# Multi-query attention on one core: first loads swapped between two queues, products of zeros on TensorE before the value products, and another cut of the last head pair

## The chip, the cores and the metric

One core of a Trainium2 chip runs the whole kernel. The metric is the time of one execution on the device in microseconds. The engines are TensorE (PE in the profile, its weight loads PEld), ScalarE (ACT), VectorE (DVE), GpSimd (POOL) and SyncE (SP). ScalarE, SyncE and GpSimd can also issue DMA transfers, each on a queue of its own.

## The reference

Eight batches, 1024 positions, 16 query heads of 64 dimensions, and one key and one value head shared by all 16 (multi-query attention). Everything is float32 in and out.

```python
q = q.transpose(0, 2, 1, 3)                       # q: (8, 1024, 16, 64)
scores = np.matmul(q, k.transpose(0, 1, 3, 2)) / np.sqrt(head_dim)
weights = np.exp(scores - np.max(scores, axis=-1, keepdims=True))
weights = weights / np.sum(weights, axis=-1, keepdims=True)
attn_out = np.matmul(weights, v)                  # k, v: (8, 1024, 64), for every head
return attn_out.transpose(0, 2, 1, 3)
```

## The kernel before

**Units of work.** Two heads of one batch make a pair, so there are 64 pairs (`NP`). A pair has eight key tiles of 128 keys (`NKT`) and two halves `c` of 512 queries. One *score* (`score`, L576) is a key tile against one half of the queries: two matmuls (L580), one for each head, on the upper and lower 64 rows of the array, into one of three PSUM slots, `sc0` to `sc2`. An exponential then reads the slot and writes fp16 weights. ScalarE does it in one instruction of 1024 elements to a partition (`exp_act`, L600). For two key tiles of most pairs (a *duo*, 54 in all) VectorE does it instead: it reads the slot with L608 (`fixed`; the planner calls it "z"), and computes a polynomial on the bits afterwards (`poly`, L626 to L643), with help from GpSimd (L652) and, in all but a few duos, from a DMA that adds (L664).

**Value products.** `value` (L671) multiplies the weights with v, in blocks of 128 queries of one head: 16 blocks in a pair (`NB`), one matmul of 128x65 for each block and key tile (L690). v has a column of ones, so the 65th column of the result is the sum of the weights. The blocks of all pairs stand in one row and are cut into groups of seven (`grouped`, L59), which are accumulated in the PSUM banks `acc0` and `acc1`; the last pair is cut by itself, into 6, 5 and 5 blocks. When a group is complete, VectorE takes the reciprocals of the sums (L699) and multiplies (L709) into `osb` in SBUF. When all 16 blocks of a pair are there, SyncE's queue sends them out as one transfer of 512 KB (L726). In the last pair nothing is sent behind the first group; after the second the first half of the rows is sent on SyncE's queue, and after the third the second half on ScalarE's (L724), 256 KB each.

**Order.** `plan` (L86) steps through a model of the engines, with a duration for each kind of work from the constants at the head of the file, and writes a list of operations in order of its model's time. The kernel emits the list as it stands, so each engine's program order is fixed. PE's next operation is chosen at L248 to L308: a score if a slot is free or will be soon (a wait of under `WAIT`, 0.5; the slot's time gets `WAKE`, 0.27, on top), else a value product. No value product is taken until the scores are `LAG`, 1.7 pairs, ahead. `nv` counts the value products so far, and `st` is the model's start of the score.

**The start.** Pair 0's keys and queries don't go through GpSimd's queue as the others do. `load_first` (L532) loads k in two halves on SyncE's queue (L539; a row of 1 KB to a partition) and q in two halves on ScalarE's (L541; four rows of 512 bytes to a partition). `cast_first(0)` (L550) casts k's first half to fp16 twice side by side on VectorE (L554), and q's first half on ScalarE (L556). `turn_first(0)` (L560) transposes both on TensorE into the banks `acc0` and `acc1` (L566, L570); VectorE copies k out (L568), ScalarE q (L572). `cast_first(1)` and `turn_first(1)` do the same with the second halves on VectorE alone (L558, L574); `turn_first(1)` stands behind the second score in TensorE's order. The third score is the first of VectorE's duo 0; it takes key tile 6, which lies in k's second half.

Of the kernel before, what the change touches and what calls it, by code (L numbers as in the profile page):

```python
# [17 lines left out]
P = 128  # L18
# [21 lines left out]
QLEAD = 3.3  # L40
LATE = 2
STOP = 1.0
REM = (4, 3, 3, 2)
Z_GAP, Z_PE, Z_ACT = 2, 2.0, 1.0
ACC_L = 0.15
# [11 lines left out]


def grouped(NP):  # L59
    cuts = list(range(0, NB * (NP - 1) + 1, NG)) + [NB * (NP - 1) + x for x in (6, 11, 16)]  # L60
    res = []
    for a, b in zip(cuts, cuts[1:]):
        segs = []
        while a < b:
            e = min(b, a // NB * NB + NB)
            segs.append((a // NB, a % NB, (e - 1) % NB + 1))
            a = e
        res.append(tuple(segs))
    return res
# [16 lines left out]
def plan(NP, NKT, stats=None):  # L86
# [85 lines left out]
    while todo_g or groups:  # L172
        if pe <= dve:
# [95 lines left out]
            if do == "qk":  # L269
                s = min(range(3), key=lambda s: slot[s])  # L270
                st = aq if slot[s] <= aq else slot[s] + WAKE
                pe, mode = st + QK_P, "qk"
                if kind == "z":
                    d, i = vunits.pop(0)
                    slot[s] = FAR
                    zs.append((st + PE_Z, s, (d, i)))
                    gap = 0
                    emit(st, "qk", duos[d][i // 2], i % 2, s)
                else:
                    u = units.pop(0)  # L280
                    na += 1
                    act = max(act, st + PE_L)
                    emit(act, "act", *u)
                    slot[s] = act + ACT_L
                    ready[u] = act + ACT_R
                    act += ACT_P
                    gap += 1
                    emit(st, "qk", *u, s)
            elif do == "av":
                st = aa  # L290
                grp, n, j = pick
                k, segs, left, a = grp
                gp, lo, hi = segs[n]
                nb = hi - lo
                pe = st + AV_B * nb
                mode = "av"
                nv += nb
                emit(st, "av", k, segs[n], j, len(left) == NKT * len(segs), a)
                left.remove((n, j))
                used[NKT * gp + j] += nb  # L300
                if not left:
                    acc[a] = FAR
                    r = pe - AV_B + PE_R
                    evs += [(r, k, segs, a, "rec"), (r, k, segs, a, "norm")]
                    groups.remove(grp)
            else:
                nxt = [x for x in slot + acc + [tav] if T < x < FAR] + [dve] * (dve > T)
                pe = max(min(nxt, default=0.0), T + 1e-3)  # L308
# [77 lines left out]
def kernel(  # L386
# [105 lines left out]
    def of_pair(x, n):  # L492
        return x[:, NKT * n : NKT * (n + 1), :]
# [38 lines left out]
    def load_first():  # L532

        st = kst.setdefault(0, {})
        st["kn"] = osb[:, 0:NKT, :]
        st["qf"] = osb[:, NB : 2 * NB, :].rearrange("p (c h) d -> p c (h d)", h=2)
        for c in range(NQC):
            x = slice(HT * c, HT * c + HT)
            nc.sync.dma_start(  # L539
                out=st["kn"][:, x, :], in_=k[0].rearrange("(p c) d -> p c d", p=P)[:, x, :])  # L540
            nc.scalar.dma_start(  # L541
                out=st["qf"][:, x, :],
                in_=q[0, :, 0:2, :].rearrange("(c p) h d -> p c (h d)", p=P)[:, x, :],
            )
        st["k16"] = osb[:, 2 * NB : 2 * NB + NKT, :].bitcast(FP16).rearrange("p c (r d) -> p c r d", r=2)
        st["k2t"] = kvp.tile([P, NKT + 1, P], FP16, tag="k2t", name="k2t0")[:, 0:NKT, :]
        place_q(0)
        load_q(0)

    def cast_first(c):  # L550
        st = kst[0]
        x = slice(HT * c, HT * c + HT)
        for r in range(2):
            nc.vector.tensor_copy(out=st["k16"][:, x, r, :], in_=st["kn"][:, x, :])  # L554
        if c == 0:
            nc.scalar.copy(out=qn[0, 0][:, x, :], in_=st["qf"][:, x, :])  # L556
        else:
            nc.vector.tensor_copy(out=qn[0, 0][:, x, :], in_=st["qf"][:, x, :])  # L558

    def turn_first(c):  # L560
        st = kst[0]
        x = slice(HT * c, HT * c + HT)
        kps = psp.tile([P, HT, P], FP16, tag="acc0", name=f"kps{c}")
        qps = psp.tile([P, HT, P], FP16, tag="acc1", name=f"qps{c}")
        for i in range(HT):
            nc.tensor.transpose(  # L566
                kps[:, i, :], st["k16"][:, HT * c + i, :, :].rearrange("p r d -> p (r d)"), ident)
        nc.vector.tensor_copy(out=st["k2t"][:, x, :], in_=kps)  # L568
        for i in range(HT):
            nc.tensor.transpose(qps[:, i, :], qn[0, 0][:, HT * c + i, :], ident)  # L570
        if c == 0:
            nc.scalar.copy(out=of_pair(qt[0], 0)[:, x, :], in_=qps)  # L572
        else:
            nc.vector.tensor_copy(out=of_pair(qt[0], 0)[:, x, :], in_=qps)  # L574

    def score(t, c, s):  # L576
        p, j = divmod(t, NKT)
# [9 lines left out]
    def score_act(t, c, s):  # L587
        score(t, c, s)
        if t not in wt:
            wt[t] = wtp.tile([P, 2, S], FP16, tag="wt", name=f"wt{t}")  # L590
# [110 lines left out]
    def normalise(k, segs):  # L701
        a, r = acc.pop(k), rec.pop(k)
        x = segs[0][0] * NB + segs[0][1]
        e = segs[-1][0] * NB + segs[-1][2]
        n = 0
        while x < e:
            y = min(e, (x // (OSB * NB) + 1) * OSB * NB)
            m = y - x
            behind["dve"] = nc.vector.tensor_tensor(  # L709
                out=osb[:, x % (OSB * NB) : x % (OSB * NB) + m, :], in0=a[:, n : n + m, 0:D],  # L710
                in1=r[:, n : n + m].unsqueeze(2).broadcast_to([P, m, D]),
                op=ALU.mult,
            )
            x, n = y, n + m
        half = NKT // 2
        for p, lo, hi in segs:
            left[p] -= hi - lo
            b, hp = divmod(p, HP)
            o = out[b, :, 2 * hp : 2 * hp + 2, :].rearrange("(c p) h d -> p c (h d)", p=P)
            s = NB * (p % OSB)  # L720
            x = osb[:, s : s + NB, :].rearrange("p (c h) d -> p c (h d)", h=2)
            if p == NP - 1 and lo > 0:
                c = slice(half, NKT) if hi == NB else slice(0, half)
                (nc.scalar if hi == NB else nc.sync).dma_start(out=o[:, c, :], in_=x[:, c, :])  # L724
            elif p < NP - 1 and left[p] == 0:
                nc.sync.dma_start(out=o, in_=x)  # L726

    ops, duos = plan(NP, NKT)
# [3 lines left out]
    for op, *args in ops:  # L732
        if op == "av":
            lasts[args[0], args[1][0]] = args[2]
    load_first()
    load_q(1)
    load_v(0)
# [6 lines left out]
    for d, ts in enumerate(duos):  # L744
        for i, t in enumerate(ts):
            units[t] = (d, 2 * i)
    with tc.manual_schedule(engines={ENG.PE, ENG.Activation, ENG.DVE, ENG.Pool, ENG.SP}):
        cast_first(0)
        turn_first(0)
        cast_first(1)  # L750
        scores = 0
        for op, *args in ops:
            if op == "qk":
                if scores == 2:
                    turn_first(1)
                scores += 1
                t, c, s = args
                if t in units:
                    d, i = units[t]
                    score_dve(t, c, s, d, i + c)  # L760
                else:
                    score_act(t, c, s)
            elif op == "act":
                exp_act(*args)
            elif op == "z":
                d, i = args
                fixed(duos[d][i // 2], i % 2)
            elif op == "step":
                poly(*args)
            elif op == "l":  # L770
                linear(*args)
            elif op == "add":
                add(*args)
            elif op == "av":
                value(*args)
            elif op == "rec":
                reciprocal(*args)
            elif op == "norm":
                normalise(*args)
            elif op == "loadq":  # L780
                load_part(*args)
            elif op == "turnq":
                trans_q(*args)
            elif op == "loadk":
                load_k(*args)
            elif op == "copyk":
                copy_k(*args)
            elif op == "turnk":
                trans_k(*args)
            elif op == "loadv":  # L790
                load_v(*args)
            else:
                raise ValueError(op)
# [28 lines left out]
```

## Time and profile before

| what | us |
|---|---|
| median of 3 runs (758.09 to 758.64) | 758.56 |
| the profiled execution | 759.06 |
| its span, from the first to the last instruction | 757.2 |
| ScalarE busy | 744.0 |
| VectorE busy | 728.2 |
| TensorE busy | 682.4 |
| first exponential starts | 6.89 |
| first value product starts | 27.55 |
| last exponential ends | 750.42 |
| last normalise ends | 752.15 |
| last transfer lands | 755.56 |

A row of a timeline has the start in us, the us that it covers, the engine (with q for an instruction that only issues), the line, the operation, out<-in and the count; in brackets stands the idle time of the engine before it and what ended it. A group of instructions has the line, engine, operation, shapes and count, then the busy us and the mean ns of one, then idle time before them. The chain of waits is followed back from the last instruction to the first. "Issue" is time in which the engine waited for nothing that the profile shows. The row PEclk tells in tenths which share of TensorE's clock the throttle granted, in 40 slices of the span.

### The profile page before, as it was taken

To read this page: it belongs to the slowest core of one execution; us is meant where nothing else is said; L and a number is where in the kernel's file an instruction comes from. 1 tells how busy PE (TensorE), PEld (TensorE's weight loads), DVE (VectorE), ACT (ScalarE), POOL (GpSimd) and SP (SyncE) were. 2 spreads that over 40 slices of the span, in tenths; PEclk is the share of its full clock that TensorE was granted. 3 is DMA by queue.
4 is the path that set the end of the run, shared out by engine and by line. 5 is a ranking of instruction groups with operands and counts; after the bars stand their busy time and mean duration, and the time that the engine had idled before them with its cause. 6 is when DMAs were issued, how large, how long until landed. Compare 5 with 4: busy or idle time off the path is not lost.

```text
span 757.2 us, 23618 instructions
## 1 busy us (share of the span) xinstructions
PE 682.4 (90%) x10256; PEld 417.7 (55%) x10256; DVE 728.2 (96%) x815; ACT 744.0 (98%) x811; POOL 401.7 (53%) x405
## 2 busy tenths in 40 slices
PE   6889899989999899999999899998999899999995
PEld 2355555555555555555555555555555555555564
DVE  5799999999999999999999999999999999999996
ACT  7999999999999999999999999999999999999996
POOL 3155556655565655666555665565555555454500
PEclk9999999999999999999999999999999999999999
DMA  9779969999999998999999999999889999966543
GB/s 172 120 121 181 209 126 197 182 186 192 166 176 170 190 194 146 187 155 196 160 186 183 161 192 182 177 192 191 167 161 167 203 155 151 179 154 127 127 99 86
DMA packets 185624, 126.18 MB, mean 167 GB/s; under 512 B 89392, under 2 KB 172464, under 8 KB 185520
## 3 DMA queue, kind: packets, MB, share of 16 engines
q0 software_dynamic: 43456, 71.97, 58.4%
q1 hardware_dynamic: 140480, 51.92, 34.9%
q8 instruction: 80, 1.31, 0.7%
q10 hardware_dynamic: 1584, 0.79, 0.4%
q14 instruction: 24, 0.20, 0.1%
HBM read 37.75 MB, written 33.55 MB: 94 GB/s over the span
## 4 chain that ended last, share of the span: by engine, by line
ACT 81%; PE 10%; issue 7%; DVE 0%; DMA 0%
ACT wt L600 81%; PE sc L580 5%; PE acc L690 5%; DMA osb<-in_q_dram 0%; DVE osb L709 0%; DVE wd L608 0%; ACT qn L556 0%; PE qps L570 0%; ACT qt L572 0%; PE kps L566 0%; DVE rec L699 0%; DVE k2t L568 0%
## 5 line engine op out<-in xcount | busy, mean ns | idle before, releaser
L600 ACT ACTIVATE wt<-sc 128x1024 f16<-128x1024 f32 x808 | 741.5, 1237 | 2.7 <-PE sc L580 2.7
L580 PE MATMUL sc<-qt,k2t 64*128 64x512 f16 x2048 | 375.4, 389 | 63.5 <-ACT wt L600 52.5
L652 POOL TENSOR_SCALAR l<-f 128x1024 f16<-128x1024 uint16 x204 | 212.9, 1044 | 222.8 <-DVE m L637 118.4
L690 PE MATMUL acc<-v,wt 128*128 128x65 f16 x6464 | 318.0, 195 | 0.6 <-issue 0.6
L690 PEld LDWEIGHTS <-wt 128*128 128x128 f16 x6464 | 237.8, 98 | 145.4 <-issue 145.2
L608 DVE TENSOR_SCALAR wd<-sc 128x1024 uint16<-128x1024 f32 x216 | 262.8, 1217 | 12.8 <-PE sc L580 11.7
L580 PEld LDWEIGHTS <-k2t 64*128 64x128 f16 x2048 | 126.9, 93 | 142.5 <-issue 93.1
L664 POOL DMA_DIRECT2D wd<-l x102 | 111.7, 1126 | 71.2 <-DVE l L639 24.1
L639 DVE TENSOR_TENSOR l<-m,l 128x2048 int16<-128x2048 f16 x108 | 128.8, 1194 | 1.0 <-POOL l L652 0.9
L637 DVE TENSOR_TENSOR m<-f,m 128x4096 f16<-128x4096 uint16 x54 | 124.0, 2297 | 0.0
L690 PE MATMUL acc<-v,wd 128*128 128x65 f16 x1728 | 103.5, 194 | 0.0
L690 PEld LDWEIGHTS <-wd 128*128 128x128 f16 x1728 | 71.2, 98 | 39.7 <-issue 39.6
L709 DVE TENSOR_TENSOR osb<-acc,rec 128x448 f32<-128x448 f32 (+4 forms) x165 | 91.3, 563 | 1.6
L629 DVE TENSOR_SCALAR m<-f 128x4096 f16<-128x4096 uint16 x54 | 67.6, 1252 | 0.2
L509 POOL DMA_DIRECT2D qn<-in_q_dram x60 | 55.7, 929 | 18.4 <-DMA qt<-qn 15.5
L626 DVE TENSOR_SCALAR f<-wd 128x4096 uint16<-128x4096 uint16 x54 | 65.4, 1211 | 0.1
L699 DVE RECIPROCAL rec<-acc 128x7 f32<-128x7 f32 (+1 forms) x147 | 28.5, 195 | 2.3 <-PE acc L690 1.7
L457 POOL DMA_DIRECT2D v<-in_v_dram x8 | 8.5, 1066 | 0.0
L643 DVE TENSOR_TENSOR wd<-wd,l 128x2048 uint16<-128x2048 uint16 x6 | 7.1, 1218 | 0.0
L463 POOL COPY k<-k 128x64 f16<-128x64 f16 x7 | 4.6, 651 | 4.4 <-DMA k<-in_k_dram 4.1
L449 POOL DMA_DIRECT2D k<-in_k_dram x7 | 5.3, 764 | 0.3
L566 PE MATMUL kps<-ident,osb 128*128 128x128 f16 x8 | 1.2, 308 | 4.0 <-DVE osb L554 4.0
(19 smaller groups left out, 16.6 us busy)
## 6 DMA issues: line engine op xcount, KB each, us to landing
wd<-l POOLq DMA_DIRECT2D x102, 512.0 KB, 6.6
out_dram<-osb SPq DMA_DIRECT2D x63, 512.0 KB, 5.9
qn<-in_q_dram POOLq DMA_DIRECT2D x63, 256.0 KB, 6.6
v<-in_v_dram POOLq DMA_DIRECT2D x8, 128.0 KB, 4.6
qt<-qn SPq DMA_TRANSPOSE x63, 4.7
k<-in_k_dram POOLq DMA_DIRECT2D x7, 128.0 KB, 6.3
osb<-in_q_dram ACTq DMA_DIRECT2D x2, 256.0 KB, 3.9
osb<-in_k_dram SPq DMA_DIRECT2D x2, 128.0 KB, 3.0
```

Of the source, the lines that this page charges most:

```text
L509: nc.gpsimd.dma_start(out=qn[g, i], in_=q[b, :, 2 * QP * r : 2 * QP * (r + 1), :].rearrange("(c p) h d -> p c (h d)", p=P)[:, n * i : n * ...
L580: nc.tensor.matmul(sc[t, c][:, h, :].rearrange("p (i x) -> p i x", x=P), keys(p // HP, h, j), queries(p, c)[64 * h : 64 * h + 64, :, :], s ...
L600: past.append(nc.scalar.activation(out=wt[t][:, :, c * QC : (c + 1) * QC], in_=sc.pop((t, c)), func=EXP, scale=ascale))
L608: behind["dve"] = nc.vector.tensor_scalar(out=wt[t].bitcast(U16)[:, :, c * QC : (c + 1) * QC], in0=sc.pop((t, c)), scalar1=vscale, scalar2 ...
L626: i = V.tensor_scalar(out=new(d, "f", U16, 1), in0=z, scalar1=1023, scalar2=None, op0=ALU.bitwise_and)
L629: i = V.tensor_scalar(out=new(d, "m", FP16, 1), in0=tmp[d, "f"], scalar1=-ONE, scalar2=1.0 / ONE, op0=ALU.add, op1=ALU.mult)
L637: i = V.tensor_tensor(out=tmp[d, "m"], in0=tmp[d, "f"], in1=tmp[d, "m"], op=ALU.mult)
L639: i = V.tensor_tensor(out=tmp[d, "l"].bitcast(I16)[:, h], in0=tmp[d, "m"][:, h], in1=tmp[d, "l"][:, h], op=ALU.mult)
L652: n = nc.gpsimd.tensor_scalar(out=tmp[d, "l"][:, x], in0=tmp[d, "f"][:, x], scalar1=GB / ONE, scalar2=GA, op0=ALU.mult, op1=ALU.add,)
L664: added.append(nc.gpsimd.dma_start(out=flat(wd[d].bitcast(I16))[:, x], in_=tmp[d, "l"].bitcast(I16)[:, x], accum_op=ALU.add,))
L690: nc.tensor.matmul(acc[k][:, n + x - lo, 0 : D + 1], w[:, h, i * P : (i + 1) * P], kst[p // HP]["v"][:, j, 0 : D + 1], start=first and x = ...
L709: behind["dve"] = nc.vector.tensor_tensor(out=osb[:, x % (OSB * NB) : x % (OSB * NB) + m, :], in0=a[:, n : n + m, 0:D], in1=r[:, n : n + m ...
```

## The change

Five parts.

1. In `load_first` k and q swap queues: q on SyncE's, k on ScalarE's.
2. The first half of q is cast by two engines, ScalarE its first two blocks of 128 and VectorE the other two; its transposes go to two banks, two blocks to `acc1`, copied out by ScalarE, and two to `sc2`, copied out by VectorE. In VectorE's order the new cast stands behind the casts of k and ahead of the copy of k, and the new copy behind the latter.
3. VectorE fills a tile of zeros at the start, 128x512 fp16, and TensorE multiplies it by itself four times (`warm`), ahead of the transposes.
4. The planner emits a "fill", one product of zeros of 512 columns into the bank `acc1`, ahead of a score whose modelled start lies over 0.3 us behind the end of TensorE's last work, from time 3.5 in the model until the first value product. A fill moves none of the model's times.
5. The last pair is cut into 6, 6 and 4 blocks, and each group's rows are sent on SyncE's queue when the group is normalised: 192, 192 and 128 KB.

```diff
+FILL_0, FILL = 3.5, 0.3
...
-    cuts = list(range(0, NB * (NP - 1) + 1, NG)) + [NB * (NP - 1) + x for x in (6, 11, 16)]
+    cuts = list(range(0, NB * (NP - 1) + 1, NG)) + [NB * (NP - 1) + x for x in (6, 12, 16)]
...
                 st = aq if slot[s] <= aq else slot[s] + WAKE
+                if nv == 0 and T > FILL_0 and st > T + FILL:
+                    emit(T, "fill")
                 pe, mode = st + QK_P, "qk"
...
+            nc.scalar.dma_start(
+                out=st["kn"][:, x, :], in_=k[0].rearrange("(p c) d -> p c d", p=P)[:, x, :])
             nc.sync.dma_start(
-                out=st["kn"][:, x, :], in_=k[0].rearrange("(p c) d -> p c d", p=P)[:, x, :])
-            nc.scalar.dma_start(
                 out=st["qf"][:, x, :],
                 in_=q[0, :, 0:2, :].rearrange("(c p) h d -> p c (h d)", p=P)[:, x, :],
             )
...
         if c == 0:
-            nc.scalar.copy(out=qn[0, 0][:, x, :], in_=st["qf"][:, x, :])
+            for i, e in ((0, nc.scalar.copy), (HT // 2, nc.vector.tensor_copy)):
+                x = slice(i, i + HT // 2)
+                e(out=qn[0, 0][:, x, :], in_=st["qf"][:, x, :])
...
+    def warm(n):
+
+        for i in range(n):
+            y = psp.tile([P, 2, QC], FP32, tag="sc2", name=f"warm{i}")
+            nc.tensor.matmul(y[:, 0, :], zeros[:, 0:P], zeros, start=True, stop=True)
+
+    def fill(i):
+
+        y = psp.tile([P, QC], FP32, tag="acc1", name=f"fill{i}")
+        nc.tensor.matmul(y, zeros[:, 0:P], zeros, start=True, stop=True)
...
-        qps = psp.tile([P, HT, P], FP16, tag="acc1", name=f"qps{c}")
+        parts = ((0, HT // 2, "acc1"), (HT // 2, HT, "sc2")) if c == 0 else ((0, HT, "acc1"),)
...
-        for i in range(HT):
-            nc.tensor.transpose(qps[:, i, :], qn[0, 0][:, HT * c + i, :], ident)
-        if c == 0:
-            nc.scalar.copy(out=of_pair(qt[0], 0)[:, x, :], in_=qps)
-        else:
-            nc.vector.tensor_copy(out=of_pair(qt[0], 0)[:, x, :], in_=qps)
+        for lo, hi, tag in parts:
+            qps = psp.tile([P, hi - lo, P], FP16, tag=tag, name=f"qps{c}_{lo}")
+            for i in range(lo, hi):
+                nc.tensor.transpose(qps[:, i - lo, :], qn[0, 0][:, HT * c + i, :], ident)
+            e = nc.scalar.copy if c == 0 and lo == 0 else nc.vector.tensor_copy
+            e(out=of_pair(qt[0], 0)[:, HT * c + lo : HT * c + hi, :], in_=qps)
...
-            if p == NP - 1 and lo > 0:
-                c = slice(half, NKT) if hi == NB else slice(0, half)
-                (nc.scalar if hi == NB else nc.sync).dma_start(out=o[:, c, :], in_=x[:, c, :])
-            elif p < NP - 1 and left[p] == 0:
+            if p == NP - 1:
+                c = slice(lo // 2, hi // 2)
+                nc.sync.dma_start(out=o[:, c, :], in_=x[:, c, :])
+            elif left[p] == 0:
                 nc.sync.dma_start(out=o, in_=x)
...
+    zeros = consts.tile([P, QC], FP16, name="zeros")
+    nc.vector.memset(zeros, 0.0)
     load_first()
...
     with tc.manual_schedule(engines={ENG.PE, ENG.Activation, ENG.DVE, ENG.Pool, ENG.SP}):
+        warm(4)
         cast_first(0)
...
+            elif op == "fill":
+                fill(scores)
```

## The prediction

> **What bounds the kernel now.** I read the shares of busy time first, then ScalarE's timeline from the start, the chain of waits over the first 36 us, the score products' mean duration in two stretches, and the last 10 us.
>
> ```profile
> PE 682.4 (90%) x10256; PEld 417.7 (55%) x10256; DVE 728.2 (96%) x815; ACT 744.0 (98%) x811; POOL 401.7 (53%) x405
> PEclk9999999999999999999999999999999999999999
> ```
> ScalarE is busy for 98% and VectorE for 96% of the span; from 60 to 600 us both are at 99 to 100%. So nothing is to be had in the middle except by starting it earlier. TensorE's clock was granted in full throughout.
>
> ```profile
> 4.29 0.62 ACT L556 CAST qn<-osb 128x512 f16<-128x512 f32 x1 [1.23 <-DMA osb<-in_q_dram]
> 5.61 0.58 ACT L572 COPY qt<-qps 128x512 f16<-128x512 f16 x1 [0.70 <-PE qps L570]
> 6.89 1.94 ACT L600 ACTIVATE wt<-sc 128x1024 f16<-128x1024 f32 x2 [0.70 <-PE sc L580]
> 9.42 22.22 ACT L600 ACTIVATE wt<-sc 128x1024 f16<-128x1024 f32 x24 [0.59 <-PE sc L580]
> 32.47 2.06 ACT L600 ACTIVATE wt<-sc 128x1024 f16<-128x1024 f32 x2 [0.83 <-PE sc L580]
> ```
> The first exponential starts at 6.89, after load, cast, transposes, copy and scores in series. Between 9.42 and 28 us ScalarE runs one exponential every 0.90 us without a stop, whatever TensorE's speed is there. Then it stalls.
>
> ```profile
> L580 PE MATMUL sc<-qt,k2t 64*128 64x512 f16 x46 | 13.1, 599 | 4.7 <-ACT wt L600 4.5
> ```
> ```profile
> L580 PE MATMUL sc<-qt,k2t 64*128 64x512 f16 x68 | 12.5, 381 | 2.4 <-ACT wt L600 1.9
> ```
> The first line is the score product in 10 to 28 us, the second in 36 to 60 us: the same instruction takes 599 ns early and 381 later. In the single records all products before 34.3 us are slow (value products follow each other every 54 ns, later every 29), and all after are fast.
>
> ```profile
> 9.42 19.38 ACT wt L600 x21
> 28.80 0.04 issue
> 28.84 0.61 PE sc L580 x2
> 29.45 0.50 PE acc L690 x7
> 29.95 0.03 issue
> 29.97 1.04 PE sc L580 x4
> 31.01 0.88 PE acc L690 x14
> 31.89 0.54 PE sc L580 x2
> 32.43 0.50 PE acc L690 x7
> 32.93 0.96 PE sc L580 x2
> 33.90 0.50 PE acc L690 x7
> ```
> Here is the cost of the slow rate: from 28.84, when value products join, the chain runs through TensorE alone until the rate doubles.
>
> ```profile
> 751.55 0.37 SPq L724 DMA_DIRECT2D out_dram<-osb  x1
> 751.65 0.49 DVE L709 TENSOR_TENSOR osb<-acc,rec 128x320 f32<-128x320 f32 x1
> 752.18 0.39 ACTq L724 DMA_DIRECT2D out_dram<-osb  x1
> ```
> ```profile
> out_dram<-osb SPq DMA_DIRECT2D x1, 256.0 KB, 2.4
> out_dram<-osb ACTq DMA_DIRECT2D x1, 256.0 KB, 3.4
> ```
> The end: after the last normalise at 752.15 a 256 KB transfer, landing 3.4 us after its issue at 755.56; the closing waits end at 757.2.
>
> **First loads and casts.** In the trace's packets k's queue (SyncE) moves its first packet at 1.78 us and q's (ScalarE) at 2.27; they land at 3.41 and 4.26. The queues are swapped. ScalarE's two issues (0.74 to 1.75) still come before its table load (ends 3.06), and SyncE has nothing else until its transposes at 7.31, so the issues cost nothing.
> If the 0.49 us belongs to the queue, q lands at 3.77 and k at 3.90. Then on VectorE: two k casts (0.50 in the rows) to 4.42, the new half cast of q (0.27, as a 128x256 cast of k) to 4.70; TensorE's k transposes 4.47 to 5.09 (0.61); k2t copy (0.43) to 5.54; the new half copy of q (half of 0.42 and a fixed part, 0.30) to 5.84; first score 5.88. ScalarE's halves (0.62 and 0.58, less 0.22 each by the slope between its 512-wide copy and its 1024-wide exponential) are done earlier. Before, it was 6.24: gain 0.36.
> If the landings stay, the path goes through q: ScalarE's half cast to 4.69, transposes to 5.33, VectorE's half copy to 5.65: gain 0.55. If k lands as late as q did (4.26), the k path ends at 6.23: gain 0. VectorE's new half cast waits for q, and the k2t copy and the second half's casts are queued behind it; these have 1.4 us of room before TensorE's second transposes at 7.21. I take a gain of **0.45**, bounds 0 and 0.55.
> The Trainium skill ("DMA: Bandwidth & Descriptors", section "Issuing engines are not separate DMA queues") says that the starting engine saves only its own issue time, as all transfers share the same DMA engines. By that rule the swap alone does nothing and the gain is 0.55; the packets' 0.49 speak for 0.36; no row here parts bytes from queue.
>
> **Four products of zeros at the start.** 512 columns at the slow rate take 0.43 us (second score pair after the first: 0.40 to 0.43): 1.7 us, behind a memset for which there is no row on VectorE (a 128x256 cast is 0.29; VectorE is idle until 3.43). They end near 3 us, before k's transposes. Cost 0; without that cover each 0.1 us of lateness is 0.1 us.
>
> **Products of zeros between scores.** The planner emits one where a score waits for its PSUM slot by over 0.3 us, from plan time 3.5 to the first value product. Counted in its list of scores, whose order the trace shows, that is nearly each ScalarE score: 18, of which 6 lie while VectorE's first four scores share the slots (trace 10.9 to 16.0), 12 after. At the slow rate one costs more than its 0.43: a score followed by full-array products leaves 0.56 between starts (33.27 to 33.83), and the way back is 0.13 more than the stream. So score plus fill is 1.11 us against a period of 0.90, and with VectorE's score among them worse: Z at 10.87, then 11.98, 13.09, Z 13.49, 14.60, 15.71 in place of 11.41, 12.33, 12.85, 13.24, 14.16. The exponentials get late by 0.46, 0.67, 1.25, 1.45, at last 2.2, and ScalarE, saturated, can't win that back. It ends when the clock rises. The row for that: TensorE ran without idle time from 29.97 and was fast at 34.3, after 4.3 us. Without idle time from about 10.05, it is fast by 14.4: **cost 1.25**. Bounds: 0 if it rises before 11, 4.7 if never (2.2 for the six, 12 x 0.21).
> The Trainium skill ("TensorE: Matmul & The Clock Gate", "Part 1: The HAM clock gate") has half rate as the default, full rate after one busy window of about 3.4 us, windows running freely. By that the rise is 3.4 to 6.8 us after the start of dense work, and the cost an estimated 0.9 to 2.0 in place of 1.25; the trace agrees as to one doubling, late, after dense work.
> Fast, a score and a fill are about 0.65 of 0.90: no further cost. In 36 to 748 us the rate stays high where under half of a stretch is streamed, so it should hold until the value products.
>
> **The stall at 28 us.** With the fast rate there, ScalarE sets the pace: the five steps from 28.51 to 34.82 took 6.31 us and take 5 x 0.90 = 4.52. **Gain 1.8**. VectorE waited 1.52, 1.13 and 1.67 us for scores in the same stretch, so it isn't late next. The first 0.59 us stall (third score behind the second half's k transposes) stays.
>
> **The end.** Blocks 6, 6, 4 instead of 6, 5, 5: the normalises are 0.56, 0.56 and about 0.43, the sum as before (1.54). Each group's rows leave on SyncE's queue at once; the last is 128 KB. SyncE's issues (0.37) fall at 750.9, 751.6, 752.2 and have only the closing waits behind them. A 256 KB transfer there lands in 2.35 (754.5); its packets took 1.07, so half the bytes save 0.5 (754.0); the transfer before may hold it by 0.2. Against 755.56: **gain 1.3**, bounds 1.0 and 1.5.
>
> **Sum**: -0.45 + 1.25 - 1.8 - 1.3 = -2.3 us. The profiled execution took 759.06 (span 757.2), so 756.8 for it; it is 0.5 above the median of 758.56, so **756.3**.
>
> **Rivals.** *Fills cost nothing*: the clock rises before or near the first fill, or fills fit the gaps. For: from 6.24 to 9.6 TensorE is nearly dense already. Against: before, that stretch raised nothing. -3.55: 755.0; with the 0.59 stall gone too, 754.4. *Absorbed*: the two saturated engines give the lead back in the middle, or the start gains only what the fills cost; the end alone remains: 757.3. Against: program order is fixed and VectorE's lead at 36 us is no smaller than ScalarE's. *Slower*: products of zeros don't raise the clock. Place: all 18 fills. Price 4.7, and the 28 us stall stays: -0.45 + 4.7 - 1.3 = +2.95, 761.5. It decides from about the eleventh fill (22 us) on slow. Against: the rate rose after work, and nothing shows that data matters. That the fills are not emitted, or too few, falls under *absorbed*.
>
> **How the numbers follow.** Forecast 0.48 (own range 755.3 to 757.2), free fills 0.25, absorbed 0.12, slower 0.10, others 0.05. About 0.2%, 1.5 us, can be told from no change here. Faster by more, below 757.0: most of the forecast's (0.41), all free fills, a little of absorbed: 0.71. Within: 0.15. Slower: 0.14. The range leaves out the lowest of free fills and the slower case: 754.4 to 758.3.
>
> **What would show it.** First exponential near 6.4; score products at 599 ns until 13 to 17 us and 381 after; exponentials over 0.90 apart between 11 and 15 us; no ScalarE wait at 32 us; the last transfer landing under 2.2 us after its issue. Wrong if the score products stay slow to 28 us, if exponentials keep 0.90 through the fills, or if the last exponential's end isn't about 1 us earlier.

## The result, and the profile after

The changed kernel's median is 755.88 us over 11 executions, against 758.56 over 11 of the kernel before: 2.7 us less. The ratio of the two, with its 95% interval, is 0.9947 [0.9925, 0.9969]. It lies lower than the ratio of the medians (0.9965) because some executions of the kernel before are 5 us and more longer, for reasons that were not looked into; below, the median of those executions is used that lie within 0.3% of a kernel's fastest (ten of eleven of the changed kernel, in the worst case five of twelve), and each kernel is set against the kernel before on its own chip. By that count the change is 2.6 us faster here, and 2.6 once more on another chip. The groups described next make differences of a few tenths between two versions uncertain. The forecast was 756.3, in a range from 754.4 to 758.3.

The profiled execution took 755.80 us, with a span of 754.0. Ten of the eleven times fall into two groups: four between 754.8 and 754.9, six between 755.8 and 756.1. The profiled one belongs to the second.

The page's busy times of the changed kernel:

```profile
PE 685.1 (91%) x10278; PEld 419.8 (56%) x10278; DVE 729.1 (97%) x818; ACT 743.3 (99%) x811; POOL 402.5 (53%) x405
```

ScalarE's timeline from the start (the bracket is the idle time ahead of a row and what ended it):

```profile
4.48 0.41 ACT L561 CAST qn<-osb 128x256 f16<-128x256 f32 x1 [1.52 <-DMA osb<-in_q_dram]
5.37 0.37 ACT L590 COPY qt<-qps 128x256 f16<-128x256 f16 x1 [0.49 <-PE qps L588]
6.59 1.94 ACT L616 ACTIVATE wt<-sc 128x1024 f16<-128x1024 f32 x2 [0.84 <-PE sc L596]
9.11 2.85 ACT L616 ACTIVATE wt<-sc 128x1024 f16<-128x1024 f32 x3 [0.58 <-PE sc L596]
12.34 2.10 ACT L616 ACTIVATE wt<-sc 128x1024 f16<-128x1024 f32 x2 [0.38 <-PE sc L596]
14.62 26.69 ACT L616 ACTIVATE wt<-sc 128x1024 f16<-128x1024 f32 x29 [0.17 <-PE sc L596]
```

The first exponential starts at 6.59 in place of 6.89. Before, ScalarE then ran through from 9.42 to 31.64 and stalled at 32.5; now it stalls between 12 and 14.6, and from there runs through past 40 us, the end of the window shown.

The chain of waits over that early stretch, start and us:

```profile
10.18 1.04 PE sc L596 x4
11.22 0.54 PE fill L574
11.76 0.54 PE sc L596 x2
12.30 0.54 PE fill L574
12.84 0.97 PE sc L596 x4
13.81 0.44 PE fill L574
14.25 0.34 PE sc L596 x2
14.59 0.02 issue
14.62 22.11 ACT wt L616 x24
```

The fills themselves stand in the chain, with 0.54, 0.54 and 0.44 us, until TensorE doubles its rate; after that ScalarE alone is the chain. TensorE's groups from 10 to 13.5 us (first line) and from 14.2 to 28 us (the other two) show the doubling, mean ns of one behind the busy time:

```profile
L596 PE MATMUL sc<-qt,k2t 64*128 64x512 f16 x10 | 2.7, 613 | 0.7 <-ACT wt L616 0.7
```
```profile
L596 PE MATMUL sc<-qt,k2t 64*128 64x512 f16 x36 | 6.8, 381 | 2.3 <-ACT wt L616 2.2
L574 PE MATMUL fill<-zeros 128*128 128x512 f16 x16 | 6.4, 398 | 0.0
```

The trace's record of the granted clock begins at 14.03 us here, and at 34.49 in the profile before: each is the moment from which the score products are fast. In what follows "the rate" is this clock of TensorE, half or full; "up" means full.

The end: DMA issues of the last 13 us, with us from issue to landing.

```profile
out_dram<-osb SPq DMA_DIRECT2D x2, 192.0 KB, 2.1
out_dram<-osb SPq DMA_DIRECT2D x1, 128.0 KB, 2.0
```

The last transfer lands at 752.79, 2.00 us after the last normalise (750.79). Before it was 755.56 and 3.41.

Exponential by exponential, the changed execution stands to the profiled one before as follows. The lead is the difference between the starts of exponentials of the same number (us, minus is earlier; further down it is given without the sign):

| place | lead | what came in between |
|---|---|---|
| exponentials 0 to 4 | -0.31 | first loads, casts, copies |
| 12 to 23 | +0.58 | fills at the slow rate: +0.89 |
| 28 to 32 | -1.22 | the stall at 28 us is gone: -1.80 |
| 60 | -0.96 | +0.26 |
| 807, the last | -1.35 | -0.39: at 650 us the execution before loses 0.66 and makes 0.27 good |
| last landing | -2.77 | the last transfer: -1.42 |
| end of the span | -3.19 | the closing waits, 1.66 to 1.24: -0.42 |

### The profile page after: what moved, and what is told of

Read it like the earlier page. It is cut to its first block, busy times and chain, and to the rows that moved or that the text cites. A ratio compares the mean times of both kernels' runs of the same rounds, so it can differ in the third digit from the quotient of the medians.

```text
span 754.0 us, 23667 instructions
## 1 busy us (share of the span) xinstructions
PE 685.1 (91%) x10278; PEld 419.8 (56%) x10278; DVE 729.1 (97%) x818; ACT 743.3 (99%) x811; POOL 402.5 (53%) x405
## 4 chain that ended last, share of the span: by engine, by line
ACT 83%; PE 8%; issue 7%; DMA 0%; DVE 0%; ACTq 0%
ACT wt L616 83%; PE sc L596 4%; PE acc L706 3%; DMA osb<-in_q_dram 0%; PE fill L574 0%; DVE osb L725 0%; PE qps L588 0%; PE kps L582 0%; DVE k2t L584 0%; ACT qn L561 0%; DVE rec L715 0%; DVE qt L590 0%; ACTq L616 0%
## 5 line engine op out<-in xcount | busy, mean ns | idle before, releaser
L596 PE MATMUL sc<-qt,k2t 64*128 64x512 f16 x2048 | 370.6, 383 | 62.5 <-ACT wt L616 51.8
L574 PE MATMUL fill<-zeros 128*128 128x512 f16 x18 | 7.6, 421 | 0.0
```

What stands on the lines that cost most here:

```text
L596: nc.tensor.matmul(sc[t, c][:, h, :].rearrange("p (i x) -> p i x", x=P), keys(p // HP, h, j), queries(p, c)[64 * h : 64 * h + 64, :, :], s ...
```

## The experiments

"To before" is the difference to the kernel before on the same chip; the changed kernel's is -2.6. The experiments ran on three chips, so a version is compared with the changed kernel through the kernel before, except where both ran on one chip.

### The fills left out

```diff
-FILL_0, FILL = 3.5, 0.3
+FILL_0, FILL = 1e9, 0.3
```

> The changed kernel without its 18 fills; all else stays. Theory (the prediction's sum): the fills cost 0.9 us while products are slow (exponentials 5 to 8) and win 1.8 back at 28 us, so they are worth 0.9 net. Without them: no delay of the exponentials up to the 23rd, score products at about 600 ns until 33 or 34 us, the stall at 28 to 34 us is back with some 1.8 us, and the time is about 0.9 above the changed kernel's: 756.8. Rival (the four products at the start and the denser start raise the rate): products fast by about 14 us here too, no stall at 28, the time 0.9 below the changed kernel's: 755.0.

To before: -1.9, so 0.7 above the changed kernel. ScalarE's timeline without fills:

```profile
6.62 1.94 ACT L616 ACTIVATE wt<-sc 128x1024 f16<-128x1024 f32 x2 [0.84 <-PE sc L596]
9.14 22.23 ACT L616 ACTIVATE wt<-sc 128x1024 f16<-128x1024 f32 x24 [0.58 <-PE sc L596]
32.20 2.06 ACT L616 ACTIVATE wt<-sc 128x1024 f16<-128x1024 f32 x2 [0.83 <-PE sc L596]
```

No delay between 9 and 28 us, the 0.83 us stall back at 32, the rate doubled at 33.97: the theory. The four products at the start raised nothing by themselves here. (Later in this profiled execution output transfers took 23 us to land, so it is read up to 40 us alone.)

### Fills only behind VectorE's first scores

```diff
-FILL_0, FILL = 3.5, 0.3
+FILL_0, FILL = 9.6, 0.3
```

> The changed kernel with fills only from model time 9.6: the six among VectorE's first four scores are left out, the twelve after them stay. Theory: with all three slots left to ScalarE a score is ready about 1 us before its use, and a slow fill takes 0.21 more than the period leaves, so the four or five until the rate rises (some 4.3 us after about 16 us, at 20 to 21 us) are covered; no delay at exponentials 5 to 8, no stall at 28 us, 0.9 below the changed kernel: 755.0, and runs less spread than the 1.3 us of the changed kernel. Rival (a slow fill costs wherever it stands): 4 or 5 exponentials late by 0.2 each, about as the changed kernel: 755.9.

754.99, to before -3.4, so 0.8 below the changed kernel, and all 11 executions between 754.8 and 755.4. In the profile exponentials 0 to 23 keep their place to 0.12 us, and there is no stall at 28. But the way there was not the one expected. Five stretches of TensorE's clock (start and end, length, then busy us of PE, PEld, DVE, ACT, POOL; PEclk is the granted share):

```profile
6.00:9.40 3.40, 3.17 (x18) 1.43 (x19) 2.19 (x7) 2.03 (x3) 0.00 (x0) 1.00 1.97 175
9.40:12.80 3.40, 1.80 (x12) 0.57 (x10) 1.93 (x2) 3.40 (x4) 0.00 (x0) 1.00 1.37 202
12.80:16.20 3.40, 2.48 (x12) 0.64 (x10) 2.30 (x2) 3.40 (x5) 2.82 (x4) 0.50 0.83 121
16.20:19.60 3.40, 3.40 (x11) 0.62 (x8) 3.33 (x4) 3.40 (x5) 0.00 (x0) 0.50 1.15 187
19.60:23.00 3.40, 3.40 (x16) 1.09 (x16) 3.37 (x3) 3.40 (x5) 0.00 (x0) 0.99 1.25 202
```

The rate had doubled already at 9.41, after a dense stretch, fell back to half at 12.82 for want of work, and doubled again at 19.65, after a stretch of late fills. (The 1.00 of the first row is no reading: the record begins with the first doubling.) Nor is it the way of every execution: in eight of the eleven the mean granted clock is 0.998 or more, against 0.995 in the profiled one, so in those the rate can't have fallen back for 6.8 us.

This suggests a reason for the two groups of the changed kernel: the rate changes only at bounds 3.41 us apart, whose place differs from one execution to the next. Where they fall so that a stretch holds the first scores from about 6 to 9.4, the rate is up before the first fill, and the fills keep it there for nothing; else it comes up later (at 13.52 to 15.71 in four profiles), and the fills cost 0.75 to 1.33 first. All four of those profiles are of the upper group. No execution of the changed kernel's lower group was profiled; the one profile of a lower group is that without the four products at the start (below), and it fits.

### k and q back on their queues

```diff
-            nc.scalar.dma_start(
+            nc.sync.dma_start(
                 out=st["kn"][:, x, :], in_=k[0].rearrange("(p c) d -> p c d", p=P)[:, x, :])
-            nc.sync.dma_start(
+            nc.scalar.dma_start(
                 out=st["qf"][:, x, :],
```

> The changed kernel with k back on SyncE's queue and q back on ScalarE's; the split casts and copies stay. Theory A (the order of landing goes by bytes and packets, not by queue, and the swap only costs): k lands at about 3.4 and q at 4.26 as before, the first exponential starts at about 6.4 in place of 6.59, time 0.2 below the changed kernel's. Theory B (the queue owns the 0.49 us between the first packets): k near 3.1 and q near 4.9, first exponential at 6.9 or later, 0.3 or more above the changed kernel. Theory C (landings move by 0.2 us from run to run): no difference beyond 0.1.

To before -2.8: 0.2 below the changed kernel, as theory A had it. k lands at 3.46 and q at 4.32, the first exponential starts at 6.45. In the profiles with the swap k lands at 3.54 to 3.71 and q at 4.38 to 4.57. In time the 0.2 did not come back: the two other pairs of versions with and without the swap (below) differ by nothing, and by 0.3 the other way. With it, k's first packet still comes first, at 1.81 us on ScalarE's queue, and q's at 2.29 on SyncE's. So the 0.49 us between them never belonged to the queue.

### The end undone

```diff
-NB * (NP - 1) + x for x in (6, 12, 16)
+NB * (NP - 1) + x for x in (6, 11, 16)
...
-            if p == NP - 1:
-                c = slice(lo // 2, hi // 2)
-                nc.sync.dma_start(out=o[:, c, :], in_=x[:, c, :])
-            elif left[p] == 0:
+            half = NKT // 2
+            if p == NP - 1 and lo > 0:
+                c = slice(half, NKT) if hi == NB else slice(0, half)
+                (nc.scalar if hi == NB else nc.sync).dma_start(out=o[:, c, :], in_=x[:, c, :])
+            elif p < NP - 1 and left[p] == 0:
```

> The changed kernel with the last pair cut 6, 5, 5 and its two 256 KB transfers on two queues, as before the change. Theory: the last transfer again lands 3.4 us after its issue in place of 2.0, the last normalise ends where it does in the changed kernel (750.8), and the time is 1.4 above the changed kernel's, up to 1.8 if the shorter closing waits (1.2 in place of 1.7 us) belong to the end too: 757.3 to 757.7. Rival (the end's gain came from a slow DMA engine in the one profile of before): under 0.7 above the changed kernel.

757.14, to before -1.25: the end is worth 1.3 us. The DMA issues of its last 13 us:

```profile
out_dram<-osb SPq DMA_DIRECT2D x1, 256.0 KB, 2.4
out_dram<-osb ACTq DMA_DIRECT2D x1, 256.0 KB, 2.6
```

So the 3.4 us from issue to landing in the profile before were not typical: there one DMA engine wrote its last word at 755.04, 0.62 us after the other fifteen. From the last normalise to the last landing it is 2.62 here and 2.00 in the changed kernel. But the closing waits take 1.66 us here, as before the change, and 1.24 to 1.25 in every profile whose last transfers all leave on SyncE's queue. 0.62 and 0.42 make 1.04; with 0.3 left over the measured 1.3 is explained only that far. Most of the 0.3 is the mix of the two groups: group against group the kernels lie 1.1 us apart (755.9 against 754.8, 757.1 against 756.0), but only two of the ten executions counted here are of the lower group, and four of the changed kernel's ten. The rival had a point as to the transfer and not as to the sum.

What held that engine up is not shown. In the profile before, an 8 KB packet of an instruction queue runs from 754.21 to 754.52, and the transfer's last ten packets of data follow one another from 754.52 on; here the corresponding 8 KB packet comes at 755.01, after the transfer. The packets don't tell which engine moved them.

### The four products at the start left out

```diff
     with tc.manual_schedule(engines={ENG.PE, ENG.Activation, ENG.DVE, ENG.Pool, ENG.SP}):
-        warm(4)
         cast_first(0)
```

> The changed kernel without the four products of zeros at the start. Theory: they end at 3.7 us, and TensorE then waits twice before the first score, so a busy stretch can only be counted from the scores (5.9 us) on; nothing changes: first exponential at 6.6, the rate doubles in some executions at about 9.4 and in most at 13.5 to 15.2, times in two groups near 754.8 and 756.0, median 755.9. Rival (they bring the doubling forward): never before 13 us here, all times near 756 to 756.5.

To before -2.4, in two groups again, 755.4 to 755.6 and 756.6 to 757.1, on a chip on which the kernel before is 0.6 slower. The profiled execution is of the lower group: the rate doubled at 8.99 and no fill delayed an exponential, as ScalarE's timeline shows:

```profile
9.07 32.21 ACT L616 ACTIVATE wt<-sc 128x1024 f16<-128x1024 f32 x35 [0.58 <-PE sc L596]
```

So the rival fell. The four products do nothing that these runs can tell.

### A dense start

```diff
-FILL_0, FILL = 3.5, 0.3
+FILL_0, FILL = 2.9, 0.3
...
-            y = psp.tile([P, 2, QC], FP32, tag="sc2", name=f"warm{i}")
+            y = psp.tile([P, 2, QC], FP32, tag=f"sc{warmed[0] % 2}", name=f"warm{warmed[0]}")
...
         nc.vector.tensor_copy(out=st["k2t"][:, x, :], in_=kps)
+        if c == 0:
+            warm(1, QC // 2)
...
             e(out=of_pair(qt[0], 0)[:, HT * c + lo : HT * c + hi, :], in_=qps)
+        if c == 0:
+            warm(1)
...
-        warm(4)
+        warm(7)
```

> The changed kernel with TensorE kept dense from 1.2 us: seven products of zeros at the start into two banks in turn (in the changed kernel four into one bank start 0.64 us apart, 0.43 of it streaming), one of 256 columns behind k's first transposes, one of 512 behind q's, and one more fill ahead of the score at 10.2. Theory (what raises the rate is one stretch of 3.4 us, at free-running bounds, streamed for over some 0.8): the rate doubles between 4.7 and 8.1 us, before the first fill among VectorE's scores, so fills cost nothing; the stall of 0.58 before the third exponential shrinks where it doubles before 7: no execution in the 756 group, median 754.6 (754.2 to 755.0). Rival (the start isn't counted, or the products delay the first score): doubling at 9.4 or later, first exponential at 6.8 or later, 755.5 or above.

To before -4.5, where the changed kernel has -2.6, on another chip. The profiled execution is one of four that took 759.9 us and more; what it lost came behind 500 us, where output transfers took 18 to 20 us to land, so it is read at the start alone. TensorE's timeline:

```profile
1.19 3.17 PE L572 MATMUL warm<-zeros 128*128 128x512 f16 x7 [1.19 <-DVE zeros L758]
4.16 0.63 PE L585 MATMUL kps<-ident,osb 128*128 128x128 f16 x4
5.83 0.60 PE L603 MATMUL sc<-qt,k2t 64*128 64x512 f16 x4 [0.17 <-DVE qt L595]
6.37 0.40 PE L585 MATMUL kps<-ident,osb 128*128 128x128 f16 x4
7.29 0.61 PE L603 MATMUL sc<-qt,k2t 64*128 64x512 f16 x4 [0.30 <-DVE k2t L587]
```

The rate doubles at 5.28; four score matmuls take 0.60 in place of 1.04 and the second transposes of k 0.40 in place of 0.61. The first exponential starts at 6.26, the third at 8.09 in place of 9.11, and no stall follows. The lead at exponential 28 is 3.19 us, where the profiled changed kernel has 1.2.

### The pieces together

> Late fills (from model time 9.6) and k and q back on their old queues, together. Theory: the two gains add: 0.9 of the late fills and some 0.15 of the earlier landings: 754.85, first exponential at 6.45. Rival (the 0.15 of the one profile is scatter): 755.0 as with late fills alone.

To before -3.4, as the late fills alone: the rival. The first exponential did start at 6.46. But in the profile the rate came up only at 20.87, and between exponentials 12 and 20 the lead shrank by 0.30, from 0.42 to 0.12: the slack of three slots doesn't cover slow fills for that long. How far that is chance, and how far the 0.2 is, these runs don't part.

> The dense start and k and q back on their old queues, together. Theory: the dense start's time less 0.15: 754.45, first exponential near 6.3 to 6.5. Rival: as the dense start alone, since its products of zeros then stand in the way of k's transposes, which can start 0.15 us sooner.

To before -4.2, against -4.5 for the dense start alone, with six of twelve executions in the count: no gain to be seen. In its profile, an execution of 778 us of which only the start is read, k landed late, at 3.73, and q at 4.59: later than in any profile with the swap.

### The changed kernel and the dense start on one chip

> The changed kernel itself, so that it stands on one chip with the three others. Theory: again two groups, one near 3.6 us below the kernel before (rate doubled at about 9.4 us, fills free) and one near 2.4 below (doubled between 13.4 and 16.9).

755.75, to before -2.6, again in two groups: 754.9 to 755.1 and 755.7 to 756.3. In the profile the rate doubled at 15.71 and the fills cost 1.33 us.

> The dense start once more, on the chip of the changed kernel. Theory: 1.5 to 2 us below the changed kernel's median, 4.2 to 4.6 below the kernel before; rate doubled between 4.7 and 8.1 us, first exponential 6.2 to 6.5, no stall before the third where it doubles before 7. Rival (a favourable chip): the gap to the changed kernel closes to under 0.7.

To before -4.0, 1.4 below the changed kernel, from five executions of twelve; the profile has the doubling at 6.40 and ScalarE busy from 6.60 without a stop past 40 us, the end of the window. The other seven took 756.3 us and more. With the longer executions taken in, the ratio to the kernel before is 0.9938 [0.9902, 0.9973], against the changed kernel's 0.9926 [0.9896, 0.9957]: no gain. So the 1.4 rests on a choice of executions. The last experiment below, with the same dense start on the same chip, bears it out as far as the dense start goes: none of its six executions is longer than the changed kernel's fastest.

### Fills of half the size

```diff
-        nc.tensor.matmul(y, zeros[:, 0:P], zeros, start=True, stop=True)
+        nc.tensor.matmul(y[:, 0 : QC // 2], zeros[:, 0:P], zeros[:, 0 : QC // 2], start=True, stop=True)
```

> The changed kernel with fills of 256 columns in place of 512. Two questions. Theory (a stretch must be streamed for over some 0.8 of 3.4 us): with VectorE's scores among them 0.78 is streamed (3 x 0.43 + 2 x 0.21 of 2.17 us), after that (0.43 + 0.21) of 0.90, 0.71; so the rate doubles at 9.4 in some executions and else not before the value products at 28 us; the stall there is back, and these executions are 0.4 to 0.9 above the changed kernel's upper group. The fills' own cost falls to 0.4 (2.17 against 1.81 for two scores, twice or three times), since they still don't fit among VectorE's scores. Rival (any use without idle time counts): doubled by 17 us, time 0.4 to 0.6 below the changed kernel's upper group.

756.6, to before -1.7: 0.9 above the changed kernel, in the theory's range for executions that aren't up by 9.4. But they got there another way. The mean granted clock of all ten executions counted is 0.990 to 0.994, against 0.998 to 1.000 for the changed kernel on this chip: after a first doubling each of them spent some 6 us or more at half rate again. So none seems to have waited for the value products to come up, and each fell back. The profiled execution, its fastest, shows how. Three stretches (PEclk is the third number from the end):

```profile
14.90:18.30 3.40, 2.38 (x16) 1.17 (x14) 3.33 (x4) 3.40 (x5) 1.02 (x2) 1.00 1.06 161
18.30:21.70 3.40, 2.35 (x12) 1.04 (x12) 3.37 (x3) 3.40 (x5) 0.00 (x0) 1.00 1.53 168
21.70:25.10 3.40, 3.22 (x11) 0.88 (x10) 3.40 (x4) 3.40 (x5) 0.40 (x1) 0.51 0.90 170
```

Up at 8.11, it fell at 21.76, when VectorE's scores had ended and a half fill and a score were all that TensorE had in 0.90 us. Two further stretches of the same work left it slow, and it came up again only at 32.0, on value products, with a stall of 0.83 us there. So the size of the fills counts twice: behind VectorE's scores, small ones neither hold the rate nor raise it.

### The dense start with late fills

```diff
-FILL_0, FILL = 2.9, 0.3
+FILL_0, FILL = 9.6, 0.3
```

The edit is to the kernel of the dense start; all else is as there.

> The dense start with fills only from model time 9.6, so none among VectorE's scores. Theory: the rate doubles between 4.7 and 8.1, falls back after one bounded stretch of 3.4 us with too little in it (by 16 us at the latest, as with the late fills alone, where it rose at 9.4 and fell at 12.8), and rises again by 20 or 21 us on the late fills: start as with the dense start, then up to 0.3 lost to slow late fills, 0 to 0.4 above the dense start. Rival (once up it holds at under half use, as it does from 36 us on): rises once, same time as the dense start.

753.88, to before -4.45, all six executions between 753.7 and 754.7. The rate is up at 4.95, falls at 11.78 and is up again at 18.60, as the theory said, but the late slow fills cost only 0.08. ScalarE's timeline up to 40 us is one row from the first exponential on:

```profile
6.10 34.94 ACT L623 ACTIVATE wt<-sc 128x1024 f16<-128x1024 f32 x38 [0.52 <-PE sc L603]
```

This is the best version that was run: 1.9 us below the changed kernel on the same chip.

## Why the prediction was right

Its sum was -2.3 us for the profiled execution; the profiles differ by 3.26, the medians by 2.7. The main mechanism was as told: the fills cost time while the rate is half, they raise it, the stall at 28 us goes, and the end gets shorter. Within the terms, the queues, the closing waits and the rule of the rate were not as told. The sizes were these.

**First loads and casts: 0.45 said, 0.30 measured.** The branch that was priced at 0.55, landings that stay where they are with the path through q, was the nearest: without the swap the first exponential starts 0.45 earlier than before. With the swap it is 0.09 to 0.36 in the profiles without the dense start; in time, the three pairs of versions don't settle whether the swap costs anything. The step that failed is the reading of the packets' 0.49 us as the queue's. The Trainium skill ("DMA: Bandwidth & Descriptors", section "Issuing engines are not separate DMA queues") was the better guide: k's packets went first on either queue.

**Fills: a cost of 1.25 said, 0.75 to 1.33 measured.** It is 0.75 in the profile whose rate doubled at 13.52, and 0.89, 1.20 and 1.33 at 14.03, 15.15 and 15.71. The forecast had 14.4 for the doubling. That it came so near was partly luck: 4.3 us of work without idle time is not the condition, and the moment shifts with the place of the bounds from one execution to the next. The first steps came as worked out: exponentials 5 to 7 were late by 0.50, 0.68 and 0.97 against 0.46, 0.67 and 1.25. *Fills cost nothing* looks to be no rival but the other group of the same kernel, four of ten executions. The sentence "before, that stretch raised nothing" took one execution's bounds for a rule: in 22 of the 53 executions counted of the kernel before, on three chips, the mean granted clock is 0.984 to 0.990, against 0.998 in the profiled one. There the rate came up early, without fills, and then was half again for some 12 to 24 us; the time is the same, as the stall at 28 us stayed. And the median falls in the upper group only because six of the ten are in it.

**The stall at 28 us: 1.8 said, 1.80 measured.** VectorE's lead at 35 us is 1.28, no smaller than ScalarE's 1.22, as assumed; in two places (47 and 62 us) VectorE gave back 0.16 each, and ScalarE with it. Why there was not tried.

**The end: 1.3 said, 1.3 measured, by two errors that cancel in part.** The 3.4 us landing that the sum started from was a straggler, which put the transfer 0.8 too high for a usual execution; and the closing waits, which the prediction took as fixed, shrank by 0.42. Between the two profiles, straggler included, the end gave 1.42 and 0.42, so 1.84. That the medians give 1.3 is luck in this term.

**The offset of 0.5 us** between the profiled execution before and its median was put down to nothing. Two things in that execution would make it longer: at 650 us it lost 0.66 against the profiles that I laid beside it and made 0.27 of it good later, and its last transfer landed 0.8 late. Together that is more than 0.5, so the offset is not accounted for.

*Absorbed* fell: the lead was kept but for 0.26. *Slower* fell, too: products of zeros raised the rate in every profile that had full ones.

As to the clock, the Trainium skill ("TensorE: Matmul & The Clock Gate", "Part 1: The HAM clock gate") has windows of 3.4 us that run freely, and one busy window as the condition. The runs agree: the changes in one profile lie whole multiples of 3.41 us apart (9.41, 12.82, 19.65; 4.95, 11.78, 18.60). Where the page has an idle window behind the fall, these traces have none: in the stretches ahead of the three falls in the first 45 us no gap of TensorE is longer than 0.8 us.

## What to carry to other kernels

An engine that is off the chain can still be slow for want of work, and the price comes due later, at the first stage that needs it: compare one instruction's mean duration early and late, not the busy share. Work that is put in to raise TensorE's rate belongs where nobody waits for TensorE, which here was the first 5 us of loads, and it has to be dense; the same products put among scores cost most of what they win until the rate is up. Count the columns in a stretch of the clock, not the busy time: full fills passed the 3000 that it took here, half fills did not. Before a last transfer's time is taken from one profile, look at whether a single DMA engine was late.

## What the runs showed of the hardware

**One count of columns raises the rate and holds it.** I cut all fourteen profiles at the bounds of 3.41 us and counted in each stretch the time in which columns stream: a matmul's columns at the rate of that stretch, 512 in 0.43 us at half rate and in 0.21 at full, and a score's two products, which run side by side, once. At half rate the 22 stretches after which the rate doubled were streamed for 0.73, and otherwise 0.77 to 0.98, of their time; the 46 after which it stayed, for up to 0.75. At full rate the stretches after which it fell had up to 0.34 (0.31 to 0.34 in the three falls of the first 45 us), and the 3002 that held it had 0.37 and more. As shares these look like two thresholds. But 3.41 us have room for 4096 columns at half rate and 8192 at full. Counted in columns the four bounds are 2980 (lowest that rose), 3070 (highest that stayed slow), 2750 (highest that fell) and 3000 (lowest that held). So one threshold of about 3000 columns in a stretch parts all cases but one or two near it, in both directions.

This fits the runs. A score in every 0.90 us is some 1900 columns in a stretch: too little to raise the rate, as in the kernel before from 17 to 24 us, and too little to hold it. With a full fill it is some 3900, enough for both. With a fill of half the size it is some 2900, just too little for both. With the late fills VectorE's scores between 9.41 and 12.82 made it 2560, and the rate fell.

The transposes of the start count in this: without them the stretch ahead of the doubling at 8.99 would be streamed for 0.53 of its time, while 0.73 without any transposes, from 10.08 to 13.49 in the profile without fills, left the rate half.

Products of zeros count as work for this: in the dense start they fill most of the stretch that ends at 5.28, and the rate doubles there.

Products into one and the same PSUM tile start 0.64 us apart at the slow rate, each waiting in the trace for the semaphore of the one before; into two tiles in turn, 0.43.
